# Scattering the expert gates once through DRAM instead of in three pieces in SBUF, in a hybrid encoder with product-key experts

## Chip, core and metric

One core of a Trainium2 chip runs the whole layer in one launch. The metric is the device time in microseconds (us), the median of the runs of one kernel.

## What is computed

One encoder layer: two token mixers, a merge, an output projection, then the part that matters here, a product-key expert layer over 512 tokens of width 1024. A query gives every token 8 heads of 16 chosen experts (128 in all) out of 16384, and a gate for each:

```python
u = w_down[ib]                      # chosen rows of 1024
act = gelu(einsum('cd,chkd->chk', xb, u)) * gb
y = einsum('chk,chkd->cd', act, w_up[ib])
```

An expert's number is i * 128 + j: i names one of 128 "expert rows", j one of 128 experts in it. A residual sum and a last RMSNorm follow.

## The kernel before

Tokens 128 to 511 (384 of them) are computed densely, against all 16384 experts, in 128 blocks of 128 experts; block i is expert row i. Tokens 0 to 127 are computed by gathering their 128 + 128 chosen weight rows per token with indirect DMAs (`fetch`, L1513), each of which brings 128 rows of 4 KB (512 KB), one per token.

A dense block has two units of work:
- `ph1` (L1437): load 512 KB of w_down, split it into two f16 halves (`wload`, L444: ScalarE L449 the high half, VectorE L452 the low), 24 matmuls of 384 columns, GELU into a slot of a ring (L1459).
- `ph2` (L1466): multiply the slot by the block's gates `Gt` (L1478), split that (L1479, L1480), load and split 512 KB of w_up, 18 matmuls of 512 columns into six PSUM banks that hold the sum over all blocks.

The gates come as lists (gij the numbers i and j, ghl the gate as two f16 halves), with the 128 chosen experts of a token along the partitions. `onehot` (L1402) turns them into a dense matrix, 16 tokens at a time: VectorE writes a one-hot over j (`ej`, L1417), a one-hot over i (`ei`, L1419) and two products of it with the gate's halves (`eg`, L1422); for each token two matmuls with `ej` as weights and `eg` moving (L1431) give G[j, i] for that token, and ScalarE copies eight tokens at a time into `Gt` (L1433). `Gt` has room for IP = 43 expert rows, so this is done in three pieces (43, 43 and 42 rows); each builds `ej` anew. A piece is a `boundary` (L1723): its 48 groups of 16 matmuls are put between the matmuls of ph1 units (12 units in the first piece, 18 in the others). No ph2 runs in a boundary, since `Gt` is being refilled.

The order of PE, VectorE and ScalarE is that of the program. `P.step` (L1379) issues the preparations (loads, splits) three units ahead. The loop at L1791 puts the 128-token work between the units by a plan: every unit has a cost for PE and VectorE, and a gathered row is worked on when the planned VectorE time has room, at most E.gcap = 1.65 rows a unit. The gathers start when the top-k of tokens 0 to 127 is done, some 19 units into this loop. All plain loads go through `E.dma` on the SP queue; gathers go through POOL's. A w_up load has two raw buffers, a w_dn load three. The ring has 13 slots in `area` (later the buffers of the gathered rows) and E.nring = 21 others; it sets how many ph1 may run ahead of ph2.

Of the kernel before, what the change touches and what calls it, by code (L numbers as in the profile page):

```python
# [11 lines left out]
F32 = mybir.dt.float32  # L12
F16 = mybir.dt.float16
# [1338 lines left out]
class Peer:  # L1352
    TD = T - 128
    NB = 128
    IP = 43
    TS = 16

    def __init__(self, E):
        self.E = E
        self.NR = E.nring  # L1360
        self.gq, self.rows = [], []
        self.yg = None
        self.owed = 0.0
        self.units, self.done, self.ready = [], 0, 0
        self.late = None

    def early(self, wp, rp, gp, bank):
        self.wp, self.bank = wp, bank
# [32 lines left out]

    def onehot(self, p, s):  # L1402

        E, IP, TS, NB = self.E, self.IP, self.TS, self.NB
        nc = E.nc
        V = nc.vector
        ts = slice(s * TS, s * TS + TS)
        nt = TS // 2
        n = min(IP, NB - p * IP)
        tiles = []  # L1410

        def prep():
            op = self.op()
            pairs = lambda x, n: x[:, ts].rearrange("p (u b) -> p u b", b=2)[:, :, None, :].to_broadcast([128, TS // 2, n, 2])
            rows = lambda a, n: self.iom[:, None, a:a + n, :].to_broadcast([128, TS // 2, n, 2])
            ej = op.tile([128, TS // 2, NB, 2], F16, name="ej", bufs=2)
            V.tensor_tensor(ej, rows(0, NB), pairs(E.gij[:, 1], NB), op=OP.is_equal)  # L1417
            ei = op.tile([128, TS // 2, IP, 2], F16, name="ei", bufs=1)[:, :, :n]
            V.tensor_tensor(ei, rows(p * IP, n), pairs(E.gij[:, 0], n), op=OP.is_equal)  # L1419
            eg = op.tile([128, 2, TS // 2, IP, 2], F16, name="eg", bufs=2)[:, :, :, :n]  # L1420
            for i in range(2):
                V.tensor_tensor(eg[:, i], ei, pairs(E.ghl[:, i], n), op=OP.mult)  # L1422
            tiles.extend((ej, eg))

        def mm(t0, tag):
            ej, eg = tiles
            o = self.bank(tag)[:, :nt * n].rearrange("p (t i) -> p t i", i=n)
            for t in range(nt):
                for i in range(2):
                    u, b = divmod(t0 + t, 2)  # L1430
                    nc.tensor.matmul(o[:, t], lhsT=ej[:, u, :, b], rhs=eg[:, i, u, :, b], start=(i == 0), stop=(i == 1))  # L1431
            t1 = s * TS + t0
            nc.scalar.copy(self.Gt[:, :n, t1:t1 + nt].rearrange("p i t -> p t i"), o)  # L1433

        return prep, lambda tag: mm(0, tag), lambda tag: mm(nt, tag)

    def ph1(self, i, gates=None, first=None):  # L1437
# [9 lines left out]
        def mm():  # L1447
# [6 lines left out]
            for k in range(KT):  # L1454
                mm3(E, o, pairs[k:k + 1], k == 0, k == KT - 1)
                for j in range(n):
                    if at[j] == k:
                        gates[j]("ba"[i % 2])
            act = lambda: E.nc.scalar.activation(self.slot(i), o, AF.Gelu_apprx_tanh, scale=UNS)  # L1459
# [6 lines left out]
    def ph2(self, i):  # L1466

        E, wp = self.E, self.wp
        nc = E.nc
        V = nc.vector  # L1470
        w = []

        def prep():
            up, scale = E.a["w_up"][i * 128:i * 128 + 128], SP / SG
# [139 lines left out]
def experts(E, ctx, fctx, rot, rpc):  # L1614
# [7 lines left out]
    with tc.manual_schedule(engines={eng.PE, eng.DVE, eng.Activation}):  # L1622
# [78 lines left out]
        R.c1.close()  # L1701
        rg, gp, pw = (cm(ctx, n, side="right") for n in ("rg", "gp", "pw"))
        P.early(pw, rg, gp, lambda tag: R.bank().rearrange("p a b -> p (a b)"))

        ops = []

        def op0():
            if not ops:
                ops.append(cm(oh, "oh", side="right"))
            return ops[0]  # L1710

        P.op = op0
        nx = 3
# [7 lines left out]
        tk.close()  # L1721
        P.main(cm(ctx, "pm"))
        def boundary(p, rest):  # L1723

            tiles = [P.onehot(p, s) for s in range(P.TD // P.TS)]
            gates = []

            def last(s):
                def mm(tag):
                    tiles[s][2](tag)  # L1730
                    if s + 2 < len(tiles):
                        tiles[s + 2][0]()
                return mm

            def first():
                tiles[0][0]()
                tiles[1][0]()

            for s, t in enumerate(tiles):
                gates += [t[1], last(s)]  # L1740
            m = len(rest) - 3
            for j, i in enumerate(rest):
                g = gates[j * len(gates) // m:(j + 1) * len(gates) // m]
                add(P.ph1(i, g, None if j else first), 3.95 + 0.4 * len(g), 1.14 + 1.25 * len(g))

        costs = [None] * len(P.units)
# [4 lines left out]

        NR = P.NR + len(P.first)
        boundary(0, range(nx, NR))
        nx = NR
        mid = len(P.units)
        for b0 in range(0, P.NB, P.IP):
            p, b1 = b0 // P.IP, min(P.NB, b0 + P.IP)
            if p:
                n = min(P.NB, b0 + P.NR)
                boundary(p, range(nx, n))  # L1760
                nx = n
            for i in range(b0, b1):
                if nx < b1 and nx < i + P.NR:
                    add(P.ph1(nx), 3.95, 1.14)
                    nx += 1
                add(P.ph2(i), 3.9, 2.2)
        last = P.units[-3:]
# [10 lines left out]
        while P.done < mid:  # L1778
            P.step()
        oh.close()  # L1780
        rpc.close()
# [5 lines left out]
        R.bg.append(topk(E, tkp, sc0, None, 0))  # L1787
        del ops[:]
        costs += [(0.0, 0.0)] * 2
        tp = td = room = 0.0  # L1790
        for k in range(mid, len(P.units)):  # L1791
# [19 lines left out]
            if k == len(P.units) - 16:  # L1811
                oh.close()
                P.final_init(cm(ctx, "fx", side="right"))
# [12 lines left out]
def body(tc, a, stage=None):  # L1826
# [4 lines left out]
    E.wr = 3  # L1831
    E.nring = 21
    E.d0, E.d1 = 2.5, 2.25
# [15 lines left out]
    with ExitStack() as ctx:  # L1849
# [10 lines left out]
        E.gates = [dp.tile([8, 128, T], F32, name=f"gates{i}") for i in range(2)]  # L1860
        E.x1 = dp.tile([4, 128, D], F32, name="x1")
        E.sc0 = dp.tile([128, 2, H, 128], F32, name="sc0d")
        E.ctx = ctx
# [27 lines left out]
```

## Time and profile before

| | us |
|---|---|
| runs: 1608.67 (median), 1607.18, 1612.53 | 1608.67 |
| profiled execution, its own time | 1611.13 |
| its span, first to last instruction | 1609.4 |
| TensorE busy in the span | 1517.9 (94%) |
| VectorE busy | 1366.2 (85%) |
| ScalarE busy | 754.0 (47%) |
| moved by DMA | 328.50 MB, mean 204 GB/s |

TensorE's 94% is an average. The table by stage among the rows below says how much of each stretch every engine was busy, which clock TensorE had (1.00 is 2.4 GHz) and how full the 16 DMA engines were. Matmuls overlap by their pipeline, so their pace is the distance of their starts, not the duration of one.

### The profile page before, as it was taken

The numbers are of one execution on the slowest core, as the hardware profiler recorded it, in microseconds if no ns is written. First come the engines' busy times: TensorE is split into PE (matmuls) and PEld (weight loads), VectorE is DVE, ScalarE is ACT, GpSimd is POOL, SyncE is SP. The second block draws the span as 40 slices with busy tenths as digits, with TensorE's granted clock in tenths as the row PEclk, the third lists the DMA queues.
The fourth block names the chain that finished last, engine by engine and source line by source line (L and its number), as shares of the span: only waits on it lengthen the run. The fifth ranks groups of instructions, "written<-read, shape, count | busy, mean of one in ns | idle before, by whom it ended". The sixth has DMA issues, their size and how long they took to land.

```text
span 1609.4 us, 29114 instructions
## 1 busy us (share of the span) xinstructions
PE 1517.9 (94%) x11401; PEld 853.4 (53%) x11401; DVE 1366.2 (85%) x2766; ACT 754.0 (47%) x1166; POOL 373.9 (23%) x300
## 2 busy tenths in 40 slices
PE   6999998799989999998999999999999999999998
PEld 3547665357675566454435665555434665544443
DVE  6788784556999997997989998989889988888886
ACT  5365757544355476442334653333334554333344
POOL 0102000000000000005442125555543114555510
PEclk9999999899999999999999999999999999999999
DMA  6533513763115424449986449999988448999873
GB/s 199 115 94 62 93 53 107 244 201 106 41 47 165 144 82 131 123 134 322 319 279 214 142 164 341 350 340 351 336 302 278 141 132 300 345 333 335 315 258 128
DMA packets 99931, 328.50 MB, mean 204 GB/s; under 512 B 11856, under 2 KB 17360, under 8 KB 99536
## 3 DMA queue, kind: packets, MB, share of 16 engines
q1 hardware_dynamic: 58688, 181.16, 34.4%
q0 software_dynamic: 39520, 142.59, 26.5%
q10 hardware_dynamic: 1584, 2.88, 0.5%
q8 instruction: 89, 1.46, 0.4%
q14 instruction: 50, 0.41, 0.1%
HBM read 315.09 MB, written 10.98 MB: 203 GB/s over the span
## 4 chain that ended last, share of the span: by engine, by line
issue 25%; DMA 14%; POOL 10%; DVE 8%; PE 4%; ACT 1%; POOLq 0%; DVEq 0%; ACTq 0%
POOL area L1520 10%; DMA area<-w_up,gidx 9%; DMA area<-w_dn,gidx 4%; DVE wlo L452 2%; PE ya L1493 1%; PE ya L1492 1%; PE ya L1491 1%; DMA raw<-w_up 1%; DVE area L1535 1%; DVE area L1527 1%; DVE Gt L1478 1%; DVE pl L1480 1%; ACT whi L449 0%; DVE eq L1127 0%; PE rps L539 0%
## 5 line engine op out<-in xcount | busy, mean ns | idle before, releaser
L452 DVE SCALAR_TENSOR_TENSOR wlo<-raw,whi 128x1024 f16<-128x1024 f32 x256 | 312.0, 1220 | 48.9 <-ACT whi L449 45.5
L449 ACT ACTIVATE whi<-raw 128x1024 f16<-128x1024 f32 x256 | 263.7, 1049 | 142.5 <-DMA raw<-w_up 108.0
L1520 POOL DMA_INDIRECT area<-w_dn,gidx x128 | 164.1, 1282 | 693.7 <-ACT whi L449 456.8
L1492 PE MATMUL ya<-wlo,ph 128*128 128x512 f16 x768 | 291.6, 380 | 6.0 <-DVE wlo L452 4.5
L1491 PE MATMUL ya<-whi,ph 128*128 128x512 f16 x768 | 292.0, 380 | 4.8 <-ACT ph L1479 4.6
L1493 PE MATMUL ya<-whi,pl 128*128 128x512 f16 x768 | 292.1, 380 | 2.6
L1520 POOL DMA_INDIRECT area<-w_up,gidx x128 | 186.7, 1458 | 231.7 <-DVE area L1535 209.0
L1479 ACT ACTIVATE ph<-Gt 128x384 f16<-128x384 f32 x128 | 66.5, 519 | 303.8 <-DVE Gt L1478 303.7
L539 PEld LDWEIGHTS <-wlo 128*128 128x128 f16 x1272 | 124.2, 98 | 115.8 <-DVE wlo L452 13.2
L1527 DVE CUSTOM_DVE_ANT_0 area<-area,h 128x1024 f32<-128x1024 f32 x128 | 156.0, 1220 | 32.2 <-DMA area<-w_dn,gidx 32.0
L538 PEld LDWEIGHTS <-whi 128*128 128x128 f16 x1272 | 124.2, 98 | 105.8 <-issue 22.0
L1535 DVE SCALAR_TENSOR_TENSOR area<-area,gco 128x1024 f32<-128x1024 f32 x128 | 164.1, 1282 | 17.7 <-DMA area<-w_up,gidx 17.5
L537 PEld LDWEIGHTS <-whi 128*128 128x128 f16 x1272 | 124.3, 98 | 91.6 <-ACT whi L481 5.5
L1493 PEld LDWEIGHTS <-pl 128*128 128x128 f16 x768 | 75.2, 98 | 116.5 <-DVE pl L1480 30.3
L537 PE MATMUL rotb<-hhl,whi 128*128 128x384 f16 x376 | 122.3, 325 | 6.4 <-ACT Gt L1433 6.4
L537 PE MATMUL rota<-hhl,whi 128*128 128x384 f16 x376 | 122.3, 325 | 6.3 <-ACT Gt L1433 5.8
L539 PE MATMUL rota<-hhl,wlo 128*128 128x384 f16 x376 | 122.5, 326 | 3.9 <-DVE wlo L452 3.9
L1491 PEld LDWEIGHTS <-ph 128*128 128x128 f16 x768 | 75.2, 98 | 94.6 <-ACT ph L1479 13.3
L539 PE MATMUL rotb<-hhl,wlo 128*128 128x384 f16 x376 | 122.5, 326 | 2.1 <-DVE wlo L452 2.0
L538 PE MATMUL rota<-hhl,whi 128*128 128x384 f16 x376 | 122.4, 326 | 0.0
L538 PE MATMUL rotb<-hhl,whi 128*128 128x384 f16 x376 | 122.4, 326 | 0.0
L1492 PEld LDWEIGHTS <-ph 128*128 128x128 f16 x768 | 75.3, 98 | 86.1 <-issue 1.0
(370 smaller groups left out, 2810.8 us busy)
## 6 DMA issues: line engine op xcount, KB each, us to landing
raw<-w_dnT SPq DMA_DIRECT2D x128, 512.0 KB
raw<-w_up SPq DMA_DIRECT2D x128, 512.0 KB
raw<-w_g SPq DMA_DIRECT2D x16, 512.0 KB
raw<-w_out SPq DMA_DIRECT2D x8, 512.0 KB
raw<-w_query SPq DMA_DIRECT2D x8, 512.0 KB
x<-x SPq DMA_DIRECT2D x8, 512.0 KB
gates<-sig POOLq DMA_DIRECT2D x14, 256.0 KB
xTs<-xT SPq DMA_DIRECT2D x8, 256.0 KB
```

Of the source, the lines that this page charges most:

```text
L449: E.nc.scalar.activation(hi, raw, AF.Copy, scale=scale)
L452: E.nc.vector.scalar_tensor_tensor(lo, raw, scale, hi, op0=OP.mult, op1=OP.subtract)
L537: E.nc.tensor.matmul(o, lhsT=lh, rhs=rh, start=start and i == 0, stop=False)
L538: E.nc.tensor.matmul(o, lhsT=lh, rhs=rl, start=False, stop=False)
L539: E.nc.tensor.matmul(o, lhsT=ll, rhs=rh, start=False, stop=stop and i == n - 1)
L1479: hi, lo = wload(E, wp, up, D, "up", 3, SU, lambda: nc.scalar.activation(ph, P, AF.Copy, scale=scale))
L1491: nc.tensor.matmul(o, lhsT=ph[:, ts], rhs=hi[:, ns], start=f, stop=False)
L1492: nc.tensor.matmul(o, lhsT=ph[:, ts], rhs=lo[:, ns], start=False, stop=False)
L1493: nc.tensor.matmul(o, lhsT=pl[:, ts], rhs=hi[:, ns], start=False, stop=l)
L1520: E.nc.gpsimd.indirect_dma_start(out=r, out_offset=None, in_=E.a[src], in_offset=bass.IndirectOffsetOnAxis(ap=E.gidx[:, k:k + 1], axis=0))
L1527: V.tensor_tensor_reduce(r, r, E.h2, op0=OP.mult, op1=OP.add, scale=1.0, scalar=0.0, accum_out=self.gact[:, k:k + 1])
L1535: self.E.nc.vector.scalar_tensor_tensor(self.yg, r, self.gco[:, k:k + 1], self.yg, op0=OP.mult, op1=OP.add)
```

## The change

The scatter is done once, for all 128 expert rows, in one stage ahead of the main loop. Per 16 tokens VectorE now makes four operations of 2048 elements (`ej`, the one-hot over i, two products); two matmuls of 128 columns per token follow (768 instead of 2304); ScalarE copies four tokens (512 columns) at a time into a staging tile `stg` of 64 tokens, of which there are two. Each full staging tile is sent to DRAM tensors `gd` by eight DMAs on the SP queue (16 expert rows each, 512 KB, in runs of 64 tokens, 256 bytes), 48 in all, two after each ph1 unit. Each ph2 reads its block's gates (128 x 384, runs of 1536 bytes, 196,608 bytes) back from DRAM by one SP load, issued two blocks ahead into one of five buffers.

`Gt` (43 x 384 floats a partition) goes; the ring grows to 35 slots. So 48 ph1 instead of 34 come before the first ph2; 19 of them ahead of the scatter as before, 25 with four-token groups ("quarters") between their matmuls, 4 (E.gtail) after it. From then on the main loop has no boundary: 14 ph2 units, then ph1 and ph2 in turn for 80 blocks, then 34 ph2. The pools of w_up's tiles and of the gate buffers are opened after the scatter's pools are closed. The core of the diff:

```diff
-    IP = 43
     TS = 16
+    TQ = 4
+    TC = 64
+    NW = 8
...
-    def main(self, mp):
-        self.Gt = mp.tile([128, self.IP, self.TD], F32, name="Gt")
+    def main(self, mp, wp, gr):
+        self.wp, self.gr = wp, gr
...
+    def write(self, n):
+        for w in self.writes[:n]:
+            w()
+        del self.writes[:n]
...
         def prep():
...
+            rows = self.iom[:, None].to_broadcast(shape)
+            ej = op.tile(shape, F16, name="ej", bufs=2)
+            V.tensor_tensor(ej, rows, pairs(E.gij[:, 1]), op=OP.is_equal)
+            eg = op.tile([128, 2] + shape[1:], F16, name="eg", bufs=2)
+            V.tensor_tensor(eg[:, 0], rows, pairs(E.gij[:, 0]), op=OP.is_equal)
+            for i in (1, 0):
+                V.tensor_tensor(eg[:, i], eg[:, 0], pairs(E.ghl[:, i]), op=OP.mult)
...
+        def mm(q):
+            if s * TS % TC == 0 and q == 0:
+                self.write(99)
+                self.stg = sg.tile([128, NB, TC], F32, name="stg", bufs=2)
             ej, eg = tiles
+            o = self.bank("")[:, :TQ * NB].rearrange("p (t i) -> p t i", i=NB)
+            for t in range(TQ):
+                u, b = divmod(q * TQ + t, 2)
                 for i in range(2):
                     nc.tensor.matmul(o[:, t], lhsT=ej[:, u, :, b], rhs=eg[:, i, u, :, b], start=(i == 0), stop=(i == 1))
+            t0 = (s * TS + q * TQ) % TC
+            nc.scalar.copy(self.stg[:, :, t0:t0 + TQ].rearrange("p i t -> p t i"), o)
+            if t0 + TQ == TC:
+                c, stg, n = s * TS // TC, self.stg, NB // self.NW
+                for w in range(self.NW):
+                    self.writes.append(lambda w=w: E.dma(E.gd[w].rearrange("i j t -> j i t")[:, :, c * TC:c * TC + TC],
+                                                         stg[:, w * n:w * n + n]))
...
+    def gload(self, i):
+        while len(self.G) <= min(i, self.NB - 1):
+            n, k = divmod(len(self.G), self.NB // self.NW)
+            self.G.append(self.gr.tile([128, self.TD], F32, name="Gb", bufs=5))
+            self.E.dma(self.G[-1], self.E.gd[n][k])
...
-            P = self.Gt[:, i % self.IP]
+            P = self.G[i]
...
+        m = n1 - nx - E.gtail
+        for j in range(m):
+            g = quarters[j * len(quarters) // m:(j + 1) * len(quarters) // m]
+            P.units.append(P.ph1(nx, g, None if j else first))
+            nx += 1
+        while P.done < len(P.units):
+            P.step()
+        P.write(99)
+        oh.close()
+        sgc.close()
+        P.main(cm(ctx, "pm"), cm(ctx, "pw", side="right"), cm(ctx, "gr", side="right"))
...
-    E.nring = 21
+    E.nring = 35
+    E.gtail = 4
```

## Rows read from the trace of the kernel before

**Rows 1.** The page's part 1: busy time of each engine, share of the span, instructions.
```profile
PE 1517.9 (94%) x11401; PEld 853.4 (53%) x11401; DVE 1366.2 (85%) x2766; ACT 754.0 (47%) x1166; POOL 373.9 (23%) x300
```
**Rows 2.** Busy time by stretch: us, PE, PEld, DVE, ACT, POOL, clock, DMA share, GB/s.
```profile
559.00:630.50 71.50, 68.65 (x1053) 47.64 (x1051) 69.03 (x100) 50.56 (x72) 0.00 (x0) 1.00 0.31 91
720.00:864.00 144.00, 132.59 (x632) 59.25 (x631) 122.00 (x176) 48.91 (x68) 66.61 (x51) 0.99 0.87 302
868.00:966.00 98.00, 92.09 (x1169) 60.72 (x1168) 90.34 (x123) 57.39 (x82) 16.32 (x11) 1.00 0.47 150
965.00:1055.00 90.00, 90.00 (x492) 47.87 (x490) 79.51 (x100) 32.49 (x47) 49.66 (x36) 1.00 0.96 345
1160.00:1238.00 78.00, 73.77 (x344) 31.30 (x343) 69.96 (x95) 29.38 (x39) 33.73 (x26) 1.00 0.88 302
1242.00:1336.00 94.00, 87.52 (x1141) 57.86 (x1139) 86.49 (x120) 54.04 (x79) 14.78 (x8) 1.00 0.43 139
1395.00:1555.00 160.00, 154.81 (x791) 75.80 (x789) 142.09 (x175) 56.50 (x82) 80.60 (x59) 1.00 0.93 328
```
**Rows 3.** The same stretch by line: first L1459 (one per ph1), then L1478 (per ph2).
```profile
965.00:1055.00 90.00, 5.73 (x12) 1.00 0.96 345
965.00:1055.00 90.00, 6.11 (x11) 1.00 0.96 345
```
**Rows 4.** Waits of the whole span: us in total, times, longest.
```profile
ACT whi L449 <- DMA raw<-w_up: 108.0, 50, 5.1
```
**Rows 5.** L1431's weight loads in each boundary: ns min/median/max, first to last start.
```profile
L1431 PEld LDWEIGHTS <-ej x768: 96/97/101, 558.7 to 629.7; 128*128 128x128 f16 x192
L1431 PEld LDWEIGHTS <-ej x768: 96/97/98, 862.3 to 960.9; 128*128 128x128 f16 x192
L1431 PEld LDWEIGHTS <-ej x768: 96/97/98, 1235.9 to 1335.5; 128*128 128x128 f16 x192
```
**Rows 6.** Timeline of PE, two stretches: start, us, operation; ten 128-column matmuls first.
```profile
349.80 0.22 PE L539 MATMUL rps<-zg,os 128*128 128x128 f16 x1
...
350.31 0.22 PE L539 MATMUL rps<-zg,os 128*128 128x128 f16 x1
...
576.58 0.57 PE L1431 MATMUL rps<-eg,ej 128*128 128x43 f16 x16
576.99 0.32 PE L537 MATMUL rps<-hhl,whi 128*128 128x384 f16 x1
577.15 0.32 PE L538 MATMUL rps<-hhl,whi 128*128 128x384 f16 x1
```
**Rows 7.** Timeline of VectorE in the first boundary: one low half, one preparation, the next.
```profile
602.99 1.22 DVE L452 SCALAR_TENSOR_TENSOR wlo<-raw,whi 128x1024 f16<-128x1024 f32 x1
604.13 1.22 DVE L1417 TENSOR_TENSOR ej<-iom,gij 128x2048 f16<-128x2048 f16 x1
605.26 0.51 DVE L1419 TENSOR_TENSOR ei<-iom,gij 128x688 f16<-128x688 f16 x1
605.81 0.94 DVE L1422 TENSOR_TENSOR eg<-ei,ghl 128x688 f16<-128x688 f16 x2
606.67 1.22 DVE L1417 TENSOR_TENSOR ej<-iom,gij 128x2048 f16<-128x2048 f16 x1
```
**Rows 8.** Instruction groups of ScalarE: busy us, mean ns; idle before, releaser.
```profile
L1433 ACT COPY Gt<-rps 128x344 f32<-128x344 f32 x48 | 36.8, 771 | 20.9 <-PE rps L1431 19.7
L403 ACT COPY sc<-ss 64x1024 f32<-64x1024 f32 x8 | 15.7, 1963 | 0.1
```
**Rows 9.** DMA queues: packets, MB, share; windows 364 to 368.5, 640 to 700, 50 to 70.
```profile
q1 hardware_dynamic: 1040, 0.52, 39.2%
q1 hardware_dynamic: 2104, 7.68, 43.5%
q0 software_dynamic: 384, 1.05, 51.9%
```
**Rows 10.** Timeline of SP's queue: the first w_up load.
```profile
476.00 0.33 SPq L1846 DMA_DIRECT2D raw<-w_up  x1
```

More of the change, by code (lines that the diff above doesn't have):

```diff
@@ L1365, in __init__, with early @@
         self.late = None
-    def early(self, wp, rp, gp, bank):
-        self.wp, self.bank = wp, bank
+        self.writes = []
+        self.G = []
+    def early(self, rp, gp, bank):
+        self.bank = bank
         self.ring = [rp.tile([128, self.TD], F32, name=f"ring{i}") for i in range(self.NR)]
@@ L1400, in sums, with onehot @@
         self.ya = [[acc.tile([128, 512], F32, name=f"ya{t}{n}") for n in range(2)] for t in range(3)]
-    def onehot(self, p, s):
-        E, IP, TS, NB = self.E, self.IP, self.TS, self.NB
+    def write(self, n):
+        for w in self.writes[:n]:
+            w()
+        del self.writes[:n]
+    def onehot(self, s, op, sg):
+        E, TS, NB, TQ, TC = self.E, self.TS, self.NB, self.TQ, self.TC
         nc = E.nc
@@ L1407, in onehot @@
         ts = slice(s * TS, s * TS + TS)
-        nt = TS // 2
-        n = min(IP, NB - p * IP)
         tiles = []
         def prep():
[L1413 to L1422, printed above, removed]
+            shape = [128, TS // 2, NB, 2]
@@ new lines, in prep @@
+            pairs = lambda x: x[:, ts].rearrange("p (u b) -> p u b", b=2)[:, :, None, :].to_broadcast(shape)
+            rows = self.iom[:, None].to_broadcast(shape)
[5 more added lines that the diff above has]
+                V.tensor_tensor(eg[:, i], eg[:, 0], pairs(E.ghl[:, i]), op=OP.mult)
@@ L1423, in prep @@
             tiles.extend((ej, eg))
-        def mm(t0, tag):
+        def mm(q):
+            if s * TS % TC == 0 and q == 0:
+                self.write(99)
+                self.stg = sg.tile([128, NB, TC], F32, name="stg", bufs=2)
             ej, eg = tiles
-            o = self.bank(tag)[:, :nt * n].rearrange("p (t i) -> p t i", i=n)
-            for t in range(nt):
+            o = self.bank("")[:, :TQ * NB].rearrange("p (t i) -> p t i", i=NB)
+            for t in range(TQ):
+                u, b = divmod(q * TQ + t, 2)
@@ new lines, in mm @@
+            if t0 + TQ == TC:
[3 more added lines that the diff above has]
+                                                         stg[:, w * n:w * n + n]))
+        return prep, mm
+    def gload(self, i):
[3 more added lines that the diff above has]
+            self.E.dma(self.G[-1], self.E.gd[n][k])
@@ L1457, in mm @@
                     if at[j] == k:
-                        gates[j]("ba"[i % 2])
+                        gates[j]()
+            if gates is not None:
+                self.write(2)
             act = lambda: E.nc.scalar.activation(self.slot(i), o, AF.Gelu_apprx_tanh, scale=UNS)
@@ L1466, in ph2 @@
     def ph2(self, i):
-        E, wp = self.E, self.wp
+        E = self.E
         nc = E.nc
@@ L1473, in prep @@
         def prep():
+            wp = self.wp
+            self.gload(i + 2)
             up, scale = E.a["w_up"][i * 128:i * 128 + 128], SP / SG
@@ L1701, in experts @@
         R.c1.close()
[L1702 to L1712, printed above, removed]
+        rg, gp = (cm(ctx, n, side="right") for n in ("rg", "gp"))
+        P.early(rg, gp, lambda tag: R.bank().rearrange("p a b -> p (a b)"))
         nx = 3
@@ L1721, in experts, with quarter, mm, first @@
         tk.close()
[L1722 to L1744, printed above, removed]
+        op = cm(oh, "oh", side="right")
+        sgc = ExitStack()
+        sg = cm(sgc, "stg")
+        tiles = [P.onehot(s, op, sg) for s in range(P.TD // P.TS)]
+        NQ = P.TS // P.TQ
+        def quarter(s, q):
+            def mm():
+                tiles[s][1](q)
+                if q == NQ - 1 and s + 2 < len(tiles):
+                    tiles[s + 2][0]()
+            return mm
+        def first():
+            tiles[0][0]()
+            tiles[1][0]()
+        quarters = [quarter(s, q) for s in range(len(tiles)) for q in range(NQ)]
+        n1 = P.NR + len(P.first)
+        m = n1 - nx - E.gtail
[9 more added lines that the diff above has]
+        P.main(cm(ctx, "pm"), cm(ctx, "pw", side="right"), cm(ctx, "gr", side="right"))
         costs = [None] * len(P.units)
@@ L1750, in add @@
             costs.append(c)
-        NR = P.NR + len(P.first)
-        boundary(0, range(nx, NR))
-        nx = NR
+        while nx < n1:
+            add(P.ph1(nx), 3.95, 1.14)
+            nx += 1
         mid = len(P.units)
[L1756 to L1766, printed above, removed]
+        for i in range(P.NB):
+            if nx < P.NB and nx < i + P.NR:
+                add(P.ph1(nx), 3.95, 1.14)
+                nx += 1
+            add(P.ph2(i), 3.9, 2.2)
         last = P.units[-3:]
@@ L1779, in experts @@
             P.step()
-        oh.close()
         rpc.close()
@@ L1787, in experts @@
         R.bg.append(topk(E, tkp, sc0, None, 0))
-        del ops[:]
         costs += [(0.0, 0.0)] * 2
@@ L1861, in body @@
         E.x1 = dp.tile([4, 128, D], F32, name="x1")
+        E.gd = [dp.tile([16, 128, T - 128], F32, name=f"gd{i}") for i in range(Peer.NW)]
         E.sc0 = dp.tile([128, 2, H, 128], F32, name="sc0d")
```

5 lines of the change are left out of this document (removed).

## The prediction

> **What bounds the kernel now.** I read the page's busy shares first [rows 1]: TensorE 94%, VectorE 85%, so TensorE looks like the bound. The table by stretch [rows 2] then shows that there are three kinds of stretch in the expert part, each with another limit. In the three boundaries (559 to 630.5, 868 to 966, 1242 to 1336) TensorE idles 3 to 7 us in each, VectorE is at 92 to 97% and the DMA engines are under half full. Where ph1 and ph2 take turns and rows are gathered (965 to 1055), TensorE is busy all 90 us, but the DMA engines are at 0.96 with 345 GB/s. There 12 ph1 and 11 ph2 ran [rows 3], so a unit takes 90 / 23 = 3.91 us, with 36 / 23 = 1.57 gathers. Where only ph2 and gathers run, TensorE idles: 11.4 us in 720 to 864, 4.2 in 1160 to 1238, and 5.2 in 1395 to 1555, which is partly such a stretch; ScalarE waits 108 us for w_up loads in all [rows 4]. So time can be won in the boundaries and in the ph2-only stretches, and the mixed stretch has no DMA time to spare.
>
> **The scatter stage.** *TensorE before.* The first and last weight load of the three pieces stand 71.0, 98.6 and 99.6 us apart [rows 5]. In them 12, 18 and 18 ph1 units ran; their 24 matmuls start 0.16 us apart [rows 6], 3.9 us a unit, so the units themselves are 46.8, 70.2 and 70.2 us. What the scatter cost is the rest: 24.2 + 28.4 + 29.4 = 82 us. *After.* 768 matmuls of 128 columns: ten such [rows 6] start 0.51 us apart from first to last, nine steps of 0.057 us, so 43.5 us, where one of 43 columns took 0.41 / 16 = 0.026 (the group of 16 before the next ph1 matmul). With 25 units of 3.9 us that is 97.5 + 43.5 = 141 us.
>
> *VectorE.* A preparation took 2.54 us from `ej` to `ej` [rows 7]. Now it has four operations of 2048 elements; the existing one starts the next after 1.13 us, so 4.5 us, 24 times: 109 us, plus 25 low halves of 1.14 us, 28 us: 137 us, of which two preparations come before the first matmul. This fits under TensorE's 141, barely. *ScalarE.* A copy of 344 columns takes 0.77 us, and another strided copy of 1024 takes 1.96 [rows 8]; the line through both gives 1.07 us at 512, pro rata at the first's pace 1.15. 96 of them are 103 to 110 us, with 25 high halves (1.05) and GELUs (0.5) 142 to 149 us by durations, which overlap by about 0.1 us each: 127 to 134. It also fits. With three engines near 90 to 100% I add the idle that TensorE had in the second boundary, about 6 us, and take 147 us, 49 beyond the units. **The scatter gives 82 - 49 = 33 us**; between the bare 141 (39) and a stage bound by ScalarE's 149 plus the same idle (25).
>
> *The writes.* 48 DMAs of 512 KB are 25.2 MB in 98,304 runs of 256 bytes. No row shows such a write. The nearest for a 128-partition transfer on the same queue is a load in 512-byte runs: 1040 packets filled 39.2% of 16 engines for 4.5 us, 27 ns each; the weight loads of 4 KB filled 43.5% of 60 us with 2104 packets, 199 ns each [rows 9]. Per byte both are 0.054 ns, so down to 512 bytes a short run shows no cost of its own, and by bytes a 256-byte run costs 13.6 ns. From above, it costs as much as the 512-byte packet, 27 ns. A farther row, 256-byte runs into 16 partitions on POOL's queue, moved 1.05 MB with 51.9% of 20 us, 101 GB/s or 40 ns per run; but few partitions and another queue may explain that, so I keep it for the tail only. A chunk of 64 tokens takes 147 / 6 = 24.5 us and contains 4.2 weight loads of 1.78 us (7.68 MB in 26.1 full us), 7.5 us. Its eight writes may take 17.0 us before they decide the stage, that is 16.6 ns a run. At 13.6 they take 13.9 us and are hidden; I take that, the nearest row's price by bytes.
>
> The Trainium skill (DMA: Bandwidth & Descriptors, Specifications) says that below 512 bytes an SDMA engine reads, modifies and writes, so line rate needs 512; that speaks against the change, and would put the run near the upper price. The same page (Why small descriptors are slow) gives 11 cycles instead of 8 for 256 bytes, which would leave it near the lower one. No run here shows which.
>
> *The changeover.* The last chunk's eight writes can only start after the last copy; behind them on SP's queue stand the first w_up loads, whose memory is also freed only then (before, the first was issued at 476 [rows 10], far ahead of its use), and the first gate load, which needs the write of its DRAM tensor. 13.9 us + 2 x 1.78 + 0.7 for the gates + some 2.5 for the first splits = 20.6 us, covered by four ph1 units, 15.6 us. **Cost 5 us**, between 0 (the writes trickle out earlier) and 20.
>
> **The main loop.** *Gate loads.* 128 loads of 0.197 MB. The first 14 have no gathers beside them; in the mixed part every pair of units has one. The plan's cap of 1.65 gathers per unit works out 256 gathers over 155 units, nearly all of the 160 mixed units, where before it also spread them over ph2-only stretches. A mixed unit then moves 2.65 x 0.524 + 0.098 = 1.49 MB. 345 GB/s at share 0.96 makes a full rate of 359 GB/s [rows 2], so 4.14 us against 3.91. **155 x 0.23 = 36 us lost**, since the rows' work stands in VectorE's order ahead of the low halves, and TensorE waits for those. The bound from below is 0, if the 0.96 hides more room; from above, at the 345 itself, 4.31 us, 62.
>
> *Stretches that go.* No ph2-only stretch has many gathers any more: after the 155 units none are left, and the last 34 ph2 run with 185 GB/s of their own. Of the 20.8 us of idle I keep 4 for the start of the gathers: **17 us won** (10 to 21).
>
> At nothing: the SP issues (some 0.3 to 0.4 us each, SP mostly waits for buffers), the longer ring, the multiply (the same operation on another tile). The gate loads come five buffers deep; without that cover each would add its landing time to a ph2. POOL's queue gets nothing new.
>
> **Sum:** -33 + 5 + 36 - 17 = -9 us. From the span of 1609.4 that is 1600.4; around it lie 1.7 us (own time 1611.13), and that execution was 2.5 us over the median of 1608.67. Against the median: 1600.
>
> **Rivals.**
> (a) *The writes decide, slower.* The 256-byte run costs 27 ns. Then a chunk needs 27.8 + 7.5 = 35.3 us of DMA instead of 24.5; with two staging tiles, copies wait for writes, and the last run lands at 24.5 + 6 x 35.3 = 236 us instead of 161. ph2 is due at 147 + 15.6 = 163, so with 4 us for loads it is 77 us late, 72 more than in the forecast: 1672. It decides from 16.6 ns on; at 20 ns the same sum gives 192 + 4 - 163 = 33, 28 more: 1628. For it speaks that no packet shorter than 512 bytes is seen to be cheaper here; against it that 512 bytes cost hardly more per byte than 4 KB. The Trainium skill's limit of 512 bytes, named above, is this rival's rule.
> (b) *The DMA keeps up, faster.* The mixed part stays at 3.91 us: -33 + 5 - 17 = -45, 1564. For it: at 0.96 TensorE had no idle. Against: 7% more bytes do not fit into 4%.
> (c) *The gain is not there:* the stage is bound by VectorE and ScalarE in turn (each at 90% and more), 160 us instead of 147: 1613.
>
> **Chances.** Forecast 0.42, its own range 1582 to 1614 (faster 0.28, same 0.12, slower 0.02). (b) 0.17, all faster. (a) at about 27 ns or more 0.21, between 17 and 27 ns 0.15, all slower. (c) 0.05, same 0.02 and slower 0.03. A measurement of this kernel tells about 0.3% (5 us) from no change. Faster 0.45, same 0.14, slower 0.41. The range takes in half of (b) and half of the slow end of (a): 1562 to 1672.
>
> **What would show it.** Right: one scatter stage of about 147 us with VectorE near 95%, no wait of the staging copies for DMA, ph2 starting about 20 us after it; then mixed stretches at a share of 0.98 or more with units of 4.1 us and VectorE waiting for gathered rows; a last stretch of ph2 with DMA near half. Wrong: `stg` copies waiting for writes, or packets of 256 bytes over 17 ns (then (a)); mixed units still at 3.91 us (then (b)).

## The result and the profile after

The changed kernel took 1622.99 us in the median of 11 runs (1614.7 to 1624.72). The kernel before, run beside it, took 1610.67 (11 runs). The ratio is 1.0075, with a 95% interval of 1.0054 to 1.0097: **0.75% slower**, some 12 us, where 1600 us and a small gain were forecast. The profiled execution had a time of its own of 1624.65 us and a span of 1622.5 us, 13.1 more than the 1609.4 of before.

The page, its busy times [rows 1], the clock and the DMA packets:

```profile
PE 1504.3 (93%) x9865; PEld 845.2 (52%) x9865; DVE 1299.7 (80%) x2574; ACT 739.1 (46%) x1118; POOL 355.0 (22%) x300
...
PEclk9999999899999998987999999999999999999999
...
DMA packets 217422, 378.64 MB, mean 233 GB/s; under 512 B 112976, under 2 KB 134864, under 8 KB 217040
```

Every engine has less work than before (TensorE 13.6 us less, VectorE 66.5), and the span is still longer: the change took work away and put waiting in its place. 50 MB more are moved, 25 out and 25 back. Three of the four slices of the clock row that are lower than nine show where: in the middle, around the new stage.

The stretches that answer to [rows 2] (us, then busy us and instructions of PE, PEld, DVE, ACT, POOL; granted clock; DMA share; GB/s): the scatter stage, the changeover to ph2, a piece of that changeover, and the mixed part:

```profile
563.00:738.00 175.00, 149.90 (x1353) 104.71 (x1351) 134.70 (x115) 122.14 (x142) 0.00 (x0) 0.92 0.67 187
738.00:778.00 40.00, 18.78 (x107) 10.14 (x106) 11.66 (x15) 11.16 (x16) 0.00 (x0) 0.74 0.86 270
740.00:756.00 16.00, 4.25 (x24) 2.18 (x24) 1.23 (x1) 0.84 (x1) 0.00 (x0) 0.75 0.82 204
880.00:1400.00 520.00, 511.71 (x2718) 262.91 (x2716) 464.16 (x590) 182.79 (x267) 275.69 (x214) 1.00 0.99 370
```

In the stage, TensorE idled 25 of 175 us, and in the changeover, 21 of 40. No other engine was full in either, and the DMA engines neither: 0.67 and 0.86. So something was waited for that none of these columns counts.

The scatter's own line, first to last weight load as in [rows 5], and the first ph2 matmul (the source views of the two lines):

```profile
L1440 PEld LDWEIGHTS <-ej x768: 96/97/151, 562.7 to 738.3; 128*128 128x128 f16 x192
...
L1515 PE MATMUL ya<-whi,ph x768: 379/379/390, 778.3 to 1615.1; 128*128 128x512 f16 x192
```

The stage lasted 175.6 us, against 147 in the forecast, and ph2 began 40.0 us after it, against 20.6. Who waited there, from 556 to 775 us (us in total, times, longest):

```profile
DVE wlo L452 <- ACT whi L449: 66.7, 10, 21.9
ACT whi L449 <- DMA raw<-w_dnT: 61.6, 7, 22.1
PEld L1440 <- issue: 26.2, 14, 8.1
PE rps L1440 <- ACT stg L1442: 23.6, 4, 7.9
PEld L537 <- ACT whi L449: 20.8, 2, 18.5
```

ScalarE waited 61.6 us, not for a write to leave its staging tile but for w_dnT: the plain 512 KB load of the next ph1. VectorE's low halves and TensorE waited behind it. (In [rows 4] the wait was for w_up; over the whole span of after, that one is down from 108.0 to 24.6 us.) Why the load was late stands on the queue that issues it. The timeline of SP's queue (start, us, operation, count), then the durations of an issue on it from 560 to 756 us (ns min/median/max):

```profile
588.40 18.05 SPq L1859 DMA_DIRECT2D gd<-stg  x8
606.54 8.16 SPq L1859 DMA_DIRECT2D raw<-w_dnT  x4
...
716.72 39.97 SPq L1859 DMA_DIRECT2D gd<-stg  x16
756.79 3.43 SPq L1859 DMA_DIRECT2D raw<-w_dnT  x3
761.15 1.32 SPq L1859 DMA_DIRECT2D Gb<-gd  x3
762.52 0.43 SPq L1859 DMA_DIRECT2D raw<-w_up  x1
```

```profile
L1859 SPq DMA_DIRECT2D gd<-stg x48: 360/2302/4005, 588.4 to 754.3; - x48
L1859 SPq DMA_DIRECT2D raw<-w_dnT x22: 327/382/2922, 567.1 to 714.9; - x22
```

A write holds SP for 2.3 us in the median, six times as long as a load of as many bytes (0.38). Eight of them in a row fill 17 to 18 us, sixteen 40 us (with 5.6 us between the two eights), and no load is issued meanwhile. It is not the issue by itself that takes so long. Of the last eight, the timeline has the first write, a later one, and the load that stands right behind them:

```profile
739.61 0.36 SPq L1859 DMA_DIRECT2D gd<-stg  x1
747.63 2.30 SPq L1859 DMA_DIRECT2D gd<-stg  x1
756.79 2.33 SPq L1859 DMA_DIRECT2D raw<-w_dnT  x1
```

The first write of each of the six eights took 0.36 to 0.38 us, though it has the same 2048 runs as the others, and a load that stands right behind an eight took 1.9 to 2.9 us. So what holds SP is the writes that were issued before. The last three w_dnT loads went out from 756.8 us on, 18.5 us after the stage had ended.

### The profile page after: what moved, and what is told of

Its sections match the earlier page's. It is cut to its first block, busy times and chain, and to the rows that moved or that the text cites. A ratio compares the mean times of both kernels' runs of the same rounds, so it can differ in the third digit from the quotient of the medians.

```text
span 1622.5 us, 26107 instructions
## 1 busy us (share of the span) xinstructions
PE 1504.3 (93%) x9865; PEld 845.2 (52%) x9865; DVE 1299.7 (80%) x2574; ACT 739.1 (46%) x1118; POOL 355.0 (22%) x300
## 4 chain that ended last, share of the span: by engine, by line
PE 29%; DMA 23%; DVE 18%; issue 13%; ACT 7%; SPq 5%; POOL 5%; ACTq 0%; POOLq 0%; DVEq 0%
DMA area<-w_up,gidx 14%; SPq L1859 5%; POOL area L1544 5%; DMA area<-w_dn,gidx 4%; PE ya L1517 3%; DVE wlo L452 3%; PE ya L1515 3%; PE ya L1516 3%; DMA raw<-w_dnT 2%; PE rps L539 2%; PE rps L537 2%; PE rps L538 2%; PE pg L537 1%; PE pg L538 1%; PE pg L539 1%
## 5 line engine op out<-in xcount | busy, mean ns | idle before, releaser
L1544 POOL DMA_INDIRECT area<-w_dn,gidx x128 | 157.0, 1227 | 720.5 <-ACT whi L449 590.8
L1503 ACT ACTIVATE ph<-Gb 128x384 f16<-128x384 f32 x128 | 66.4, 518 | 409.6 <-DVE Gb L1502 409.6
L1544 POOL DMA_INDIRECT area<-w_up,gidx x128 | 175.0, 1367 | 160.1 <-DVE area L1559 141.7
L537 PEld LDWEIGHTS <-whi 128*128 128x128 f16 x1272 | 125.6, 99 | 118.7 <-ACT whi L449 21.5
L537 PE MATMUL rps<-hhl,whi 128*128 128x384 f16 x384 | 127.9, 333 | 20.0 <-ACT whi L449 20.0
L539 PE MATMUL rps<-hhl,wlo 128*128 128x384 f16 x384 | 127.7, 332 | 1.7 <-DVE wlo L452 1.7
L538 PE MATMUL rps<-hhl,whi 128*128 128x384 f16 x384 | 127.8, 333 | 0.0
L539 PE MATMUL rotb<-hhl,wlo 128*128 128x384 f16 x320 | 105.2, 329 | 3.6 <-DVE wlo L452 3.5
L539 PE MATMUL rota<-hhl,wlo 128*128 128x384 f16 x320 | 104.4, 326 | 3.9 <-DVE wlo L452 3.9
L537 PE MATMUL rotb<-hhl,whi 128*128 128x384 f16 x320 | 105.1, 328 | 0.2 <-ACT whi L449 0.2
```

The lines of the kernel that those rows point to most:

```text
L537: E.nc.tensor.matmul(o, lhsT=lh, rhs=rh, start=start and i == 0, stop=False)
L538: E.nc.tensor.matmul(o, lhsT=lh, rhs=rl, start=False, stop=False)
L539: E.nc.tensor.matmul(o, lhsT=ll, rhs=rh, start=False, stop=stop and i == n - 1)
L1544: E.nc.gpsimd.indirect_dma_start(out=r, out_offset=None, in_=E.a[src], in_offset=bass.IndirectOffsetOnAxis(ap=E.gidx[:, k:k + 1], axis=0))
```

## The experiments

Twelve kernels ran, each timed beside the kernel before. The *stage* is first to last weight load of the scatter; the *hole* is from there to the first ph2 matmul, of which four ph1 units are 15.6 us; a *mixed unit* is 520 us x 21 matmuls a unit / the matmuls counted between 880 and 1400 us (by the same count two stretches of before, 965 to 1155 us, give 3.91, as [rows 3] does by units).

| kernel | us | ratio to before | stage | hole | mixed unit |
|---|---|---|---|---|---|
| after | 1623.0 | 1.0075 [1.0054, 1.0097] | 175.6 | 40.0 | 4.02 |
| x1 without writes | 1572.2 | 0.9748 [0.9716, 0.9781] | 142.2 | 20.5 | 4.05 |
| x2 writes on POOL's queue | 1596.0 | 0.9905 [0.9877, 0.9933] | 148.0 | 33.6 | 4.04 |
| x3 four ph1 prepared early | 1624.7 | 1.0095 [1.0067, 1.0124] | 175.8 | 37.2 | 4.01 |
| x4 long runs, loads of 4 blocks, x3's edit | 1590.8 | 0.9897 [0.9858, 0.9936] | 142.1 | 28.1 | 4.10 |
| x5 = x4, cap 1.45 | 1563.1 | 0.9712 [0.9681, 0.9742] | 142.1 | 27.7 | 3.89 |
| x6 = x4, pools in another order | 1587.8 | 0.9863 [0.9832, 0.9895] | 142.1 | 22.6 | 4.10 |
| x7 only five gate loads | 1622.0 | 1.0067 [1.0042, 1.0091] | 176.9 | 39.8 | 4.02 |
| x8 short runs on the read side | 1578.8 | 0.9817 [0.978, 0.9855] | 142.2 | 24.3 | 4.01 |
| x9 = x6, six row buffers | 1554.6 | 0.9676 [0.9645, 0.9707] | 142.1 | 22.5 | 3.89 |
| x10 = x8 with x3's, x5's, x6's edits | 1565.4 | 0.9732 [0.9705, 0.9759] | 142.1 | 23.5 | 3.89 |
| x11 after, cap 1.45 | 1607.2 | 0.9983 [0.9964, 1.0001] | 175.7 | 41.9 | 3.89 |
| x12 before, cap 1.45 | 1618.5 | 1.0072 [1.0045, 1.01] | | | |

### The writes: x1, x2, x3

x1 takes the writes away:

```diff
-                    self.writes.append(lambda w=w: E.dma(E.gd[w].rearrange("i j t -> j i t")[:, :, c * TC:c * TC + TC],
-                                                         stg[:, w * n:w * n + n]))
+                    self.writes.append(lambda: None)
...
-            self.E.dma(self.G[-1], self.E.gd[n][k])
+            i0 = (len(self.G) - 1) * 128
+            self.E.dma(self.G[-1], self.E.a["w_dn"][i0:i0 + 128, :self.TD])
```

> Leaves out: the 48 writes of the gates; each gate load reads the first 384 columns of 128 rows of w_down instead, in runs of the same 1536 bytes. Theory S (the short-run writes hold SP's queue, about 2.3 us each, and the weight loads wait behind them): the scatter stage falls from 176 to about 147 us and the 19 us hole before the first ph2 goes, so about 1623 - 29 - 20 = 1574 us. Rival E (three engines near their limits bind the stage, the writes only go along): the stage stays near 170 us and only the hole goes, about 1600.

It took 1572.2 us. The scatter's line and the stage of x1, in the views shown of after:

```profile
L1440 PEld LDWEIGHTS <-ej x768: 96/97/100, 565.9 to 708.1; 128*128 128x128 f16 x192
```

```profile
566.00:708.00 142.00, 141.10 (x1358) 100.92 (x1357) 134.62 (x115) 124.56 (x143) 0.00 (x0) 1.00 0.28 90
```

Without the writes the stage is what the bare sum of matmuls said (141): TensorE is busy 141.1 of 142 us at full clock, VectorE 134.6. So the writes cost 1623 - 1572 = 51 us, and the trace places 53: 175.6 - 142.2 = 33 in the stage, and 40.0 - 20.5 = 20 in the hole. Rival E of the expectation, a stage that stays near 170 us without them, is out.

x2 leaves all bytes and runs as they are and issues the writes from POOL:

```diff
-                    self.writes.append(lambda w=w: E.dma(E.gd[w]...
+                    self.writes.append(lambda w=w: nc.gpsimd.dma_start(E.gd[w]...
```

> The 48 writes are issued on POOL's queue instead of SP's, same runs of 256 bytes, same bytes. Theory S: SP's loads are free, the stage is about 150 us, and the hole shrinks to the wait for the last writes' gates, 5 to 10 us: 1575 to 1590 us. Rival D (the DMA engines themselves are too slow on 256-byte runs, whoever issues them): the weight loads get their turn but staging buffers come free no earlier than now; stage 165 to 175 us, 1605 to 1620. Rival E: stage unchanged, about 1605 to 1623.

1596.0 us, 27 less than after, and 6 above the range of Theory S: the stage came as expected, the hole did not. The issues of x2 on POOL, from the line's source view, and the DMA view of 600 to 735 us (queue: packets, MB, share of 16 engines):

```profile
L1446 POOL DMA_DIRECT2D gd<-stg x48: 1152/1152/1179, 592.3 to 724.0; - x48
```

```profile
q0 software_dynamic: 6298, 22.92, 71.6%
q1 hardware_dynamic: 3353, 12.23, 24.2%
```

An issue takes 1.15 us here, and it isn't in front of the loads. The 22.92 MB are 89,500 runs of 256 bytes; 71.6% of 16 engines for 135 us makes **17.3 ns a run**. In after, where nothing but writes moved:

```profile
DMA packets 12808, 3.27 MB, mean 204 GB/s; under 512 B 12807, under 2 KB 12807, under 8 KB 12807
...
q1 hardware_dynamic: 12807, 3.25, 81.4%
```

That is 740 to 756 us in the DMA view: 0.814 x 16 x 16 us / 12807 = **16.3 ns a run**. So the run costs the DMA engines nearly the same from either queue, and x2 fills them (0.96 in all) where after leaves a third of their time unused in its stage (0.67). What x2 removes is the loads' place behind the writes on SP. It doesn't remove the hole: there VectorE waits for the first gate load. And some staging copies now wait for a write to leave their tile, which in after none did. Two of x2's waits from 556 to 790 us:

```profile
DVE Gb L1502 <- DMA Gb<-gd: 15.1, 1, 15.1
...
ACT stg L1442 <- DMA gd<-stg: 11.6, 3, 5.6
```

The Trainium skill (DMA: Bandwidth & Descriptors, Issuing engines are not separate DMA queues) says that issuing from several engines saves only the sequencer's time, "which is usually small relative to the DMA itself". The engine times of 16.3 and 17.3 ns agree that it is the same 16 engines. The 27 us differ from the rest of it: in a burst SP was held 2.3 us a write, and with it every load behind.

x3 issues the loads and splits of the four ph1 after the scatter ahead of the last writes:

```diff
-        while P.done < len(P.units):
+        ng = len(P.units)
+        while nx < n1:
+            P.units.append(P.ph1(nx))
+            nx += 1
+        while P.done < ng:
             P.step()
```

> Order alone: the four ph1 that follow the scatter are put into the list before it is drained, so their weight loads are issued two units ahead of the last eight writes instead of behind them. Theory S: the hole of 19 us falls to about 5 to 8, the stage stays at 176 us: about 1610 us. Rivals D and E: D the same as S; E no opinion on the hole, 1610 to 1623.

This missed: 1624.7, as slow as after. x3's waits from 556 to 775 us, and its writes on SP:

```profile
ACT whi L449 <- DMA raw<-w_dnT: 45.0, 5, 10.4
...
DVE Gb L1502 <- DMA Gb<-gd: 22.5, 1, 22.5
```

```profile
L1863 SPq DMA_DIRECT2D gd<-stg x48: 377/2338/3994, 586.7 to 758.6; - x48
```

The longest wait for a load went from 22.1 us in after to 10.4, and a wait of 22.5 us for the gates came in its place. The hole is set by the last writes themselves, issued until 758.6: whatever is put ahead of them, the gates can be read only when they have landed.

### The length of a run: x4, x6, x8

x8 turns the DRAM layout, so that a partition's 16 rows x 64 tokens are one run of 4 KB in a write, and the short runs (256 bytes) are on the loads:

```diff
-                    self.writes.append(lambda w=w: E.dma(E.gd[w].rearrange("i j t -> j i t")[:, :, c * TC:c * TC + TC],
-                                                         stg[:, w * n:w * n + n]))
+                    self.writes.append(lambda w=w: E.dma(E.gd[w][c], stg[:, w * n:w * n + n]))
...
-            self.E.dma(self.G[-1], self.E.gd[n][k])
+            self.E.dma(self.G[-1].rearrange("p (c t) -> p c t", t=self.TC), self.E.gd[n][:, :, k].rearrange("c j t -> j c t"))
...
-        E.gd = [dp.tile([16, 128, T - 128], F32, name=f"gd{i}") for i in range(Peer.NW)]
+        E.gd = [dp.tile([6, 128, 16, 64], F32, name=f"gd{i}") for i in range(Peer.NW)]
```

> The turned DRAM layout with one-block loads: writes in runs of 4 KB, each of the 128 gate loads in 768 runs of 256 bytes, so the short runs are moved from the writes to the loads. The stage is 142 us as in x4, hole about 20 us (the four ph1 are not put early here). If a 256-byte run costs SP 1.15 ns wherever it stands, a load holds SP for 0.9 us per block, which SP has; what matters is whether the engines pay: at 16 ns a run a load takes 0.77 us of all engines instead of 0.55, so the saturated mixed part gets 80 x 0.2 = 18 us longer: 1605 to 1615. If the engines do not pay, 1590 to 1598.

1578.8 us, below both ranges of the expectation. The scatter and the writes of x8, source views:

```profile
L1440 PEld LDWEIGHTS <-ej x768: 95/97/100, 561.6 to 703.8; 128*128 128x128 f16 x192
...
L1858 SPq DMA_DIRECT2D gd<-stg x48: 326/1175/1619, 587.4 to 712.5; - x48
```

The same bytes in 128 runs instead of 2048 hold SP for 1.2 us, and the stage is back at the 142 us of a kernel without writes. The short runs on the load side (128 loads of 768) raise the DMA share of the mixed part to 1.03 at 372 GB/s, and a mixed unit takes 4.01 us, no more than in after. They are cheap there; x10, which has the same loads, runs units of 3.89 us. An issue of one takes 0.38 us in the median, not the 0.9 that the expectation worked out. That it is so because they come spread out, one load for two units, is likely and not shown.

x4 has the same writes, x3's edit, and loads of four blocks at once in runs of 1 KB, in two buffers:

```diff
-            self.G.append(self.gr.tile([128, self.TD], F32, name="Gb", bufs=5))
-            self.E.dma(self.G[-1], self.E.gd[n][k])
+            g = self.gr.tile([128, 6, 4, self.TC], F32, name="Gb", bufs=2)
+            self.E.dma(g, self.E.gd[n][:, :, k:k + 4].rearrange("c j i t -> j c i t"))
+            self.G += [g[:, :, j] for j in range(4)]
```

> The DRAM layout is turned: each write is 4 KB per partition in one run, and gates are read back four blocks at a time in runs of 1 KB (32 loads of 786 KB into two buffers), with the four ph1 put early as in x3. Same bytes, 6144 + 24,576 runs instead of 98,304 + 16,384. Theory S and rival D: writes cost SP 0.3 us and the engines their bytes (1.5 to 1.8 us), stage 147 to 152 us, hole under 6 us: 1570 to 1580. Rival E: the stage stays near 170: 1595 to 1605.

It gave the stage of 142.1 us too, but 1590.8 in all, 11 above what was expected: its mixed unit takes 4.10 us, the longest of all (with x6, which has the same loads), and its hole is 28.1. Why the large loads make the unit longer was not tested; with two more row buffers (x9, below) the same loads go with units of 3.89 us. Compared with x8, whose loads are a quarter as large, the longer runs gained nothing.

In x4 the first gate load was issued at 720.8 us, 9 after the last write, whose staging memory the buffers take over. x6 opens the two pools in the other order, so that w_up's tiles get that memory:

```diff
-        P.main(cm(ctx, "pm"), cm(ctx, "pw", side="right"), cm(ctx, "gr", side="right"))
+        P.main(cm(ctx, "pm"), gr=cm(ctx, "gr", side="right"), wp=cm(ctx, "pw", side="right"))
```

> x4_long_runs_4 with the pool of the gate buffers opened before that of w_up's tiles, so that the gate buffers take the one-hots' memory and do not lie on the staging tiles. If the hole of 12 us before the first ph2 is the gate load waiting for the memory of the last eight writes (all of them), the load goes out some 8 us earlier and the hole falls to 3 to 5 us: 1582 to 1585. If it waits for the data of its own DRAM tensor, nothing changes: 1591.

1587.8: the hole fell from 28.1 to 22.6 us, so the memory had a part in it. The time fell by 3, where 6 to 9 were expected, less than the spread of x4's runs (1589.1 to 1600.2).

### The mixed part: x7, x5, x11, x12, x9

A mixed unit had grown from 3.91 to 4.02 us. x7 tests whether the gate loads do it, as the prediction had it (Theory M in the expectations):

```diff
-        while len(self.G) <= min(i, self.NB - 1):
+        while len(self.G) < 5:
...
-            P = self.G[i]
-            V.tensor_tensor(P, self.slot(i), P, op=OP.mult)
+            P = self.slot(i)
+            V.tensor_tensor(P, P, self.G[i % 5], op=OP.mult)
```

> The changed kernel with only the first five gate loads; every block uses one of these five tiles, unchanged, and the product is written to the ring slot. Leaves out 123 of the 128 gate loads. Theory M (their 24 MB are what slows the mixed part): mixed units 3.91 to 3.95 us instead of 4.03, 12 to 19 us less than the changed kernel: 1604 to 1611. Rival L: 1618 to 1623.

1622.0, and the mixed stretch of x7 beside that of after above:

```profile
880.00:1400.00 520.00, 509.77 (x2714) 262.71 (x2712) 465.41 (x591) 182.95 (x267) 285.00 (x215) 1.00 0.96 347
```

Without 123 of the 128 loads the engines moved 347 instead of 370 GB/s, and did 2714 instead of 2718 matmuls. **The bytes of the gate loads cost nothing that can be measured**, and Theory M fell. Another reading of after's mixed part was needed. Its waits from 880 to 1400 us:

```profile
POOL area L1544 <- DVE area L1559: 118.4, 86, 3.2
POOL area L1544 <- DVE gact L1551: 97.6, 80, 2.2
DVE area L1559 <- DMA area<-w_up,gidx: 29.3, 33, 1.8
...
DVE area L1551 <- DMA area<-w_dn,gidx: 23.0, 27, 1.8
```

VectorE works 464.2 us and waits 29.3 + 23.0 for gathered rows: 516.5 of 520 us are gone in its order. And POOL, which issues the gathers, waits mostly for VectorE to give back one of the four row buffers. The rows go in a circle: a gather can't be issued before a buffer is free, and VectorE can't go on before it lands. At 1.65 rows a unit the circle has to bring a row each 2.4 us. That is Theory G of the expectations. A lower cap on the rows of a unit (x5, x11) or more buffers (x9) should help it; fewer bytes should not.

x5 is x4 with a cap of 1.45; x11 and x12 are after and before with the same edit:

```diff
-    E.lead, E.gcap = 1.0, 1.65
+    E.lead, E.gcap = 1.0, 1.45
```

> x4_long_runs_4 with E.gcap 1.45 instead of 1.65: the 256 gathers are spread over 176 units instead of 155. Theory M (the mixed part is bound by DMA bytes: 4.03 us a unit at 370 GB/s instead of 3.91): 2.45 x 0.524 + 0.098 = 1.38 MB a unit is 3.7 us at 370, so the mixed units go back to 3.91 us and 10 to 19 us are won against x4's 1591: 1572 to 1581. Rival L (the mixed part loses to something else, such as the order of rows and halves on VectorE): 1586 to 1591.

> The changed kernel with E.gcap 1.45 alone. Theory G: mixed units 3.9 instead of 4.02 us, 17 to 25 us won: 1598 to 1606, so still with the stage and the hole of the short-run writes, but faster than before. If the gain in x5 came from large gate loads meeting gathers: under 8 us, 1615 or more.

> The kernel before with E.gcap 1.45 alone, a control: its mixed stretches are short (22 pairs) and lost little, its ph2-only stretches hold 1.2 to 1.4 gathers a unit already, and the last rows no longer fit the plan (12 are left for the end). Theory G: within 5 us of before, 1605 to 1615. If the cap is simply too high for any loop, 1590 to 1600.

x5 took 1563.1, 28 less than x4, where Theory M gave 10 to 19; x11 1607.2, 16 less than after, just short of the 17 to 25 expected, and no clear gain on before. The mixed stretch of x5 and of x11, and x5's two waits for rows there:

```profile
880.00:1400.00 520.00, 520.00 (x2807) 274.31 (x2805) 456.92 (x575) 196.06 (x277) 267.08 (x197) 1.00 0.97 359
```

```profile
880.00:1400.00 520.00, 520.00 (x2806) 274.40 (x2805) 456.26 (x579) 196.11 (x276) 274.34 (x197) 1.00 0.98 362
```

```profile
DVE area L1560 <- DMA area<-w_up,gidx: 15.0, 18, 2.7
...
DVE area L1552 <- DMA area<-w_dn,gidx: 8.5, 10, 2.0
```

VectorE now has 457 + 23.5 = 480 of 520 us taken, and TensorE doesn't wait. In the kernel before, the same cap does harm (x12: 1618.5, a little outside what was expected). Its gathers don't fit any more before the last unit. The wait in x12 from 1395 us to the end that shows it:

```profile
PEld L1491 <- ACT ph L1479: 26.5, 1, 26.5
```

So a cap of 1.45 is no gain of its own: it pays where the loop is uniform and has units left for the rows that it puts off, and that room the change had made (this last is argued from the plan; no run varies it alone).

x9 is x6 with the cap of 1.65 and two more row buffers:

```diff
+        self.more = [mp.tile([128, D], F32, name=f"row{i}") for i in range(2)]
...
-        while self.gq and len(self.rows) < 4:
+        while self.gq and len(self.rows) < 6:
...
-            r = self.area[:, self.nrow % 4 * D:self.nrow % 4 * D + D]
+            b = self.nrow % 6
+            r = self.area[:, b * D:b * D + D] if b < 4 else self.more[b - 4]
```

> x6_pools_swapped (cap 1.65) with six buffers for gathered rows instead of four. Theory G (the mixed part loses to the turnaround of a gather: four buffers, each used, refilled and landed in some 9 us, allow 2.3 to 2.4 us a row, which is what the cap of 1.65 a unit asks, so VectorE waits for rows and delays the halves): two more buffers bring mixed units from 4.03 to 4.10 us back to 3.9, x6's 1588 falls to 1560 to 1572. Rival B (the DMA engines' rate is the limit whatever the number of buffers): 1584 to 1590.

1554.6 us, 33 less than x6 and below the range expected, **the best of all: 0.9676 [0.9645, 0.9707] of before**. The mixed stretch of x9, and x6's two waits for rows in the same stretch:

```profile
880.00:1400.00 520.00, 520.00 (x2808) 274.66 (x2807) 483.24 (x605) 197.77 (x279) 319.42 (x221) 1.00 1.01 387
```

```profile
DVE area L1560 <- DMA area<-w_up,gidx: 31.0, 28, 2.6
DVE area L1552 <- DMA area<-w_dn,gidx: 29.4, 29, 2.7
```

The same 1.65 rows a unit (221 in 2808 / 21 units), *more* bytes a second than ever (387 GB/s), and units of 3.89 us. x9 has no wait of VectorE for a gathered row in this stretch. The DMA engines had the room all along; the four buffers kept them from using it. Theory G stands.

### Put together: x10

x10 is x8 with the early ph1 of x3, the order of pools of x6 and the cap of 1.45.

> Turned layout with one-block loads (short runs on the loads), tail put early, pools swapped, cap 1.45. From x8's 1579: the hole some 5 us shorter, the mixed part without its loss, 15 to 20 us: 1553 to 1560. If the short-run loads fill the engines too far for the cap to help (share 1.03 in x8), 1565 to 1572.

1565.4, above the range of 1553 to 1560: the hole came out at 23.5 us where x8 had 24.3, so the edits to the hole gained nothing over x8, and the cap gave 13 where it gave 28 on x4. Part of what the cap gave x4 was thus owed to x4's own slow units (4.10 against 4.01). The time lies in the second range, but not for its reason: the engines were not too full for the cap to help, for the units are 3.89 us. x8's layout with six row buffers was not tried.

## Why the prediction was wrong, step by step

**The reading of before** held for the boundaries and the ph2-only stretches: time could be won there. That "the mixed stretch has no DMA time to spare" did not hold; x9 shows it.

**The scatter's matmuls, VectorE and ScalarE: right.** 141 us bare and 147 with idle were forecast; with the writes left out (x1) or in 4 KB runs (x4 to x6, x8 to x10) it is 142.1 to 142.2, so the 6 us of idle did not come. (24 starts 0.16 us apart make 3.84 us, not 3.9; the shortest mixed units measured are 3.89, so nothing hangs on it.) A preparation was to take 4.5 us; the groups of after have two operations of 1.217 and two of 1.225 us, 4.9 by durations. A copy of 512 columns was to take 1.07 to 1.15 us and took 1.078. Rival (c), a stage bound by VectorE and ScalarE, is out.

**"At nothing: the SP issues (some 0.3 to 0.4 us each, SP mostly waits for buffers)": this step failed**, and with it the direction. An issue by itself did cost that: 0.36 to 0.38 us for the first write of each eight. But SP issued one after the other, and the term left out that it is held while earlier writes are under way: 2.3 us for each write that follows, 17 to 18 us for eight, some 104 us for all 48, with the loads of the next units behind them. The forecast added writes and loads up as work of the same engines, and never asked which stands behind which.

The price of a run on the DMA engines was bounded with care. The forecast took 13.6 ns and said that the writes decide from 16.6 on; the engines were busy for 16.3 to 17.3, and with the issue moved away (x2) the stage took 148.0 us. On SP the engines were busy only 0.81 of the time while nothing but writes moved. So a run took 16 us x 16 / 12807 = 20 ns of elapsed time, and eight writes 20.5 us, where the forecast had 13.9 and allowed 17.0. The stage took 175.6, **29 us more than forecast**. Whether the writes under way wait for their 2048 runs to be made out or to be moved, these runs don't tell apart; that the engines were busy only 0.81 speaks for the first.

By 4 KB runs, which moved at up to 418 GB/s in x4's writes, 256 bytes would take 9.8 ns of one of 16 engines, so 16.3 is 1.7 times the price by bytes. The Trainium skill (DMA: Bandwidth & Descriptors, Specifications and Why small descriptors are slow) warns of runs under 512 bytes, and this trace agrees; its 11 cycles for 8 would make, as an estimate, 1.4 times.

**The changeover: 5 us forecast, 24.4 measured** (40.0 - 15.6), a little over the upper bound of 20. The forecast took the last eight writes at 13.9 us; the first gate load was issued 21.5 us after the first of them (739.6 and 761.2), three loads of the four ph1 meant to cover them stood behind them, and the granted clock was 0.74 in the mean of the 40 us, between its two levels of 1.2 and 2.4 GHz, after TensorE had waited. Without the writes (x1) the changeover is 20.5 - 15.6 = 4.9 us, the 5 of the forecast; as x1 leaves out the writes that the forecast counted in, that agreement is luck.

**Gate loads in the mixed part: +36 forecast, about +14 measured, and not by them.** By [rows 3]'s way of counting, 75 ph1 and 75 ph2 ran in 600 us (880 to 1480): 4.00 us a unit instead of 4.14, and 155 x 0.09 = 14 (17 by the 4.02 of the matmuls). x7 shows that the gate loads have no part in it. The step that failed here is the full rate of 359 GB/s, worked out from a share of 0.96: x9 moved 387 for 520 us. A stretch's share and rate did not say what the engines could do when asked for more.

**Stretches that go: -17 forecast, about -16 measured.** Of the 20.8 us that TensorE idled in such stretches of before, 5 are left in after: none in the first ph2 units, 4.2 where the gathers start (4 were kept for that) and 1 in the last ph2 units:

```profile
778.00:835.00 57.00, 57.00 (x270) 26.23 (x269) 54.53 (x231) 23.31 (x36) 0.00 (x0) 1.00 0.61 206
835.00:880.00 45.00, 40.81 (x213) 20.73 (x212) 36.44 (x59) 13.82 (x19) 12.40 (x11) 0.98 0.65 228
1477.00:1605.00 128.00, 127.05 (x588) 57.14 (x587) 80.88 (x112) 52.54 (x74) 2.64 (x2) 1.00 0.62 211
```

With the measured terms the sum is (175.6 - 97.5) - 82 = -4, +24, +14 and -16: +18, against +13 measured in the spans. With x1's stage and hole it is -37 + 5 + 14 - 16 = -34, against 1574.7 - 1609.4 = -35; by x1's own mixed unit of 4.05 the third term would be some 7 more. So the terms account for the spans to within some 8 us.

**The rivals.** Rival (a) had the side and nearly the time (1628 at 20 ns, which is the elapsed price above; by the engines' 17.3 ns its sum would give 1612) with a mechanism one step off: its staging copies wait for writes, which in after none did. The writes decide by the queue that they are issued on. Rival (b), in which the mixed part stays at 3.91, was right that the DMA engines had room and wrong on the unit and the result; that x5 comes to its 1564 takes a lower cap besides long runs. Of the signs named beforehand, a share of 0.99, units of 4.0 us and VectorE waiting for rows came true and led to the wrong cause; "packets of 256 bytes over 17 ns" stood just at its border; that loads might wait on SP was not among them.

## What to carry to other kernels

Price a DMA three times: the bytes, the runs on the DMA engines, and the time that a burst of its kind holds the queue that it stands on; then list what is queued behind it. Put the short runs of a transposing round trip on the side that is spread out in time (x8), or the burst on a queue where no load is waiting (x2; 27 us here instead of x8's 44). And when a ring of buffers feeds an engine, read who waits for whom around the ring before blaming bandwidth: two more buffers were worth 33 us here (x6 to x9), and the bytes nothing.

## What was not expected of the hardware

- An issue of 512 KB on SP took 0.33 to 0.38 us as a load of 4 KB runs, about 1.2 in a burst of writes in 4 KB runs (x4, x8), and 2.3 in a burst of writes in 256-byte runs; the first write of a burst took 0.33 to 0.39 in either form. On POOL it took 1.15 us for the same 256-byte runs, every time.
- The writes from POOL's queue appear as packets of 22.92 MB / 6298 = 3.6 KB, those from SP's as packets of 256 bytes; the DMA engines' time per run was nearly the same (17.3 and 16.3 ns).
- The DMA engines moved 387 GB/s over 520 us in x9, where the mixed stretch of [rows 2] had 345 at a share of 0.96.
